# In-projection in two chunks of 1024 columns instead of four of 512

## The chip, the cores and the metric

The kernel runs on one core of a Trainium2 chip. TensorE multiplies matrices (PE in the profile; PEld is its loading of the stationary operand), VectorE (DVE), ScalarE (ACT) and GpSimd (POOL) do the elementwise work, and SyncE (SP) issues most transfers. The metric is the device time of one execution in microseconds; lower is better. Times are compared as medians of several runs, and one execution is profiled instruction by instruction.

## The reference

One encoder layer on 1024 tokens of width 1024, all in float32. Only its first step is changed here:

```python
hn = rms_norm(x, norm1_g)
proj = hn @ w_in                      # (1024, 1024) @ (1024, 2304): qA 512 | kA 128 | vA 128 | qB 512 | kB 512 | vB 512
qa, ka = rope(rms_norm(qa, gain)), rope(rms_norm(ka, gain))   # per head of 64
qb, kb = rms_norm(qb, gain), rms_norm(kb, gain)
```

After it come dense attention for group A (8 query heads on 2 key heads), a mixture of dilated window attentions for group B, an output projection with two RMSNorms, and a GEGLU MLP with a centred width-3 convolution. The row factor of the first RMSNorm isn't applied to x: the norms of q and k take it up in their epsilon, and v is scaled by it later. The column gain norm1_g is multiplied into the weights.

## The kernel before

**Precision.** Each float32 operand is split into a high part (ACT copies it into a rounded type) and a low part (DVE subtracts). A product is three matmuls: high x high, high x low, low x high. So each k-tile of 128 rows and each tile of 128 tokens costs three matmuls, with 128x128 of x as the stationary operand and the weights as the moving one.

**Strassen-Winograd products.** The kA and vA columns (256) are done first, in plain form, one tile of 128 tokens after the other (`kv_proj`, L287). The other four blocks of 512 columns are `CHUNKS`: kb, vb, qa, qb. In each chunk tokens, inner dimension and columns are halved, and seven products of halves with sums and differences of blocks (`prods`, L240) replace the eight block products. A product therefore has 512 tokens (4 tiles), 4 k-tiles and 256 columns: 4 x 4 x 3 = 48 matmuls of 256 moving columns; the four chunks have 28 products. The x side is prepared once (`x_sums`, L256, and `s_split`, which splits them), the weight side for each product (`w_prep`, L392: a difference of two blocks on DVE, a copy on ACT, a subtraction on DVE, 1024 columns each) into one of three buffers, two products ahead. Weights arrive in two transfers of 1 MB per chunk (`w_load`) and are scaled by norm1_g in place, on ACT, the first two pieces on GpSimd (`w_scale`, L381).

**Results.** A product fills 1024 columns of PSUM (two banks); there are three such groups (`in_group`, L412). `in_out` (L434) copies or adds it into the chunk's quadrants c11 to c22, with DVE or ACT on 1024 columns at a time and two of the first chunk's sums on GpSimd. When a quadrant is final, `done` (L471) yields its next steps: for kb a square, mean, root, norm and the store to a scratch in DRAM; for vb the scaling and the store; for qa a norm and the rotary turn (a table and eight small products on GpSimd, then two DVE operations); for qb the norm. The three last sums of the qb chunk and the later query norms are put into the attention's loop as `late` and `spread` steps (from L1283), tied to a place there by an operand.

**The mean square of x** is summed from eight row tiles of x loaded beside the transposed x (`n_load`, L263; `n_sq`, L266) through two buffers.

**Order.** The loop over m (L1194) writes the steps down in one order. A planner of the framework then orders each engine's queue from that order and from its own estimate of when operands are ready; each engine takes its queue strictly in turn. So an instruction whose operand comes later than planned holds up what is queued behind it on its engine. The attention's first groups follow directly: `a_main_bounded` (L721), scores, exponential on ACT, split, product with v. Its first group needs the rotated queries of tokens 0 to 511, heads 0 to 3, transposed on TensorE by the steps in `prep`.

The kernel holds a second form of the attention for data outside a bound, which isn't executed with these inputs.

Of the kernel before, what the change touches and what calls it, by code (L numbers as in the profile page):

```python
# [27 lines left out]
CHUNKS = (("kb", 1280), ("vb", 1792), ("qa", 0), ("qb", 768))  # L28
# [35 lines left out]
F_TMP = O_F  # L64
F_UA = O_F + 1024
F_WA = (O_F + 2048, O_F + 4096)
F_WC = O_F + 6144
F_XN = (O_F, O_F + 4096)
F_KVT = O_F + 5120
F_KSQ = O_F + 4096  # L70
# [66 lines left out]
def tile_encoder_layer(ctx, tc, x, xT, w_in, w_kv, gains, norm1_g, norm2_g, w_out, w_up, convs,  # L137
# [14 lines left out]
    def emit(bounded):  # L152
# [85 lines left out]

        chunks = [(at, kind) for kind, at in CHUNKS]
        prods = [(c, n) for c in range(4) for n in ((1, 5, 2, 7, 6, 3, 4) if c else (1, 2, 5, 7, 6, 3, 4))]  # L240
# [7 lines left out]

        def x_load_t(tt):
            dma(f(qab(tt), 1024), xT[:, tt, :])  # L250

        def x_prep(tt):
            for half in range(2):
                split(a_op(((1, 2), (3, 4))[tt // 4][half], tt % 4), f(qab(tt) + 512 * half, 512))

        def x_sums(tt):  # L256
            q0, q1 = qab(tt), qab(tt + 4)
            vec.tensor_tensor(f(q1 + 512, 512), f(q1, 512), f(q1 + 512, 512), op=OP.add)
            vec.tensor_tensor(f(q1, 512), f(q0, 512), f(q1, 512), op=OP.subtract)
            vec.tensor_tensor(f(q0, 512), f(q1 + 512, 512), f(q0, 512), op=OP.subtract)  # L260
            vec.tensor_tensor(f(q0 + 512, 512), f(q0 + 512, 512), f(q0, 512), op=OP.subtract)

        def n_load(tt):  # L263
            dma(f(F_XN[tt % 2], 1024), perm_rows(x, tt, D))

        def n_sq(tt):  # L266
            act(bank(4, 1024), f(F_XN[tt % 2], 1024), AF.Square, accum_out=f(SM_SS1 + tt, 1))
            if tt < 6:
                n_load(tt + 2)

        def s_split(n, t):
            raw = {5: qab(t + 4) + 512, 7: qab(t + 4), 6: qab(t), 3: qab(t) + 512}[n]
            split(a_op(n, t), f(raw, 512))


        def kv_load(half):
            dma(f(F_WC + 1024 * half, 1024), w_kv[half])

        def kv_split(k):
            o, raw, g = R_A[7] + 2048 * (k // 4) + 256 * (k % 4), f(F_WC + 256 * k, 256), f(SM_G1 + k, 1)  # L280
            act(r(o, 256), raw, AF.Copy, scale=g)
            vec.scalar_tensor_tensor(r(o + 1024, 256), raw, g, rf(o, 256), op0=OP.mult, op1=OP.subtract)

        def kv_bank(tt):
            return tt
# [16 lines left out]
        def kv_out(i):  # L302
            stg = F_KVT + 256 * (i % 3)
            act(f(stg, 256), bank(kv_bank(i), 256), AF.Copy)
            dma(kvscr[i], f(stg, 256))


        def k_fetch():
            dma(heads(f(F_TMP, 1024), 8), kvscr[:, :, 0:128].rearrange("t p c -> p t c"))

        def k_norm():
            k3, t = heads(f(F_TMP, 1024), 16), F_KSQ + 1024
            act(f(F_KSQ, 1024), f(F_TMP, 1024), AF.Square)
            vec.tensor_reduce(f(t, 16), heads(f(F_KSQ, 1024), 16), axis=AX.X, op=OP.add)
# [4 lines left out]
            vec.tensor_tensor(k3, k3, f(t, 16)[:, :, None].to_broadcast([128, 16, 64]), op=OP.mult)  # L319
            vec.tensor_tensor(k3, k3, fp(O_GA + 128, [0, 16], [1, 64]), op=OP.mult)  # L320

        def k_turn():
            for ax in range(2):
                for half in range(2):
                    gp.tensor_tensor(fp(F_KSQ + 32 * ax + 16 * half, [128, 8], [64, 2], [1, 16]),
                                     fp(F_TMP + 32 * ax + 16 * (1 - half), [128, 8], [64, 2], [1, 16]),
                                     fp(F_ROPE + 64 + 32 * ax + 16 * half, [128, 8], [0, 2], [1, 16]), op=OP.mult)

        def k_add():
            k4 = fp(F_TMP, [128, 8], [64, 2], [1, 64])  # L330
            vec.tensor_tensor(k4, k4, fp(F_ROPE, [128, 8], [0, 2], [1, 64]), op=OP.mult)
            vec.tensor_tensor(f(F_TMP, 1024), f(F_TMP, 1024), f(F_KSQ, 1024), op=OP.add)

        def k_split():
            src = fp(F_TMP, [64, 16], [1, 64])
            h, l = (64, 0) if bounded else (0, 64)
            act(rp(R_KNA + h, [128, 16], [1, 64]), src, AF.Copy)
            vec.tensor_tensor(rp(R_KNA + l, [128, 16], [1, 64]), src, rfp(R_KNA + h, [128, 16], [1, 64]), op=OP.subtract)
# [12 lines left out]

        def v_fetch():
            gp.memset(fp(F_VA + 64, [66, 16], [1, 2]), 1.0)
            for kv in range(2):
                dma(fp(F_VA + 66 * kv, [132, 8], [1, 64]),
                    kvscr[:, :, 128 + 64 * kv:192 + 64 * kv].rearrange("t p c -> p t c"))

        def v_scale():
# [3 lines left out]
            for t in range(8):  # L362
                v = fp(F_VA + 132 * t, [66, 2], [1, 64])
                act(v, v, AF.Copy, scale=f(SM_SS1 + t, 1))
            if bounded:
                act(r(R_VA, 1056), f(F_VA, 1056), AF.Copy)
                vec.tensor_tensor(r(R_VA + 1056, 1056), f(F_VA, 1056), rf(R_VA, 1056), op=OP.subtract)
# [7 lines left out]
        def w_buf(c, half):  # L375
            return F_WC if half else F_WA[c % 2]

        def w_load(c, half):
            dma(f(w_buf(c, half), 2048), w_in[c, half])

        def w_scale(c, half):  # L381
            for k in range(4):
                o, g = f(w_buf(c, half) + 512 * k, 512), f(SM_G1 + 4 * half + k, 1)
                if c or half or k > 1:
                    act(o, o, AF.Copy, scale=g)
                else:
                    gp.tensor_scalar(o, o, g, None, op0=OP.mult)

        def w_op(m):
            return R_WR + 2048 * (m % 3)  # L390

        def w_prep(m):  # L392
            if m >= len(prods):
                return
            c, n = prods[m]
            b11, b12, b21, b22 = [fp(w_buf(c, half) + 256 * u, [512, 4], [1, 256]) for half in range(2) for u in range(2)]
            eng = vec
            if n == 5:
                vec.tensor_tensor(b11, b12, b11, op=OP.subtract)
            elif n == 7:  # L400
                eng.tensor_tensor(b12, b22, b12, op=OP.subtract)
            elif n == 6:
                eng.tensor_tensor(b11, b22, b11, op=OP.subtract)
            elif n == 4:
                eng.tensor_tensor(b11, b21, b11, op=OP.subtract)
            src = {2: b21, 3: b22, 7: b12}.get(n, b11)
            o = w_op(m)
            h = rp(o, [256, 4], [1, 256])
            act(h, src, AF.Copy)
            vec.tensor_tensor(rp(o + 1024, [256, 4], [1, 256]), src, rfp(o, [256, 4], [1, 256]), op=OP.subtract)  # L410

        def in_group(m):  # L412
            c, n = prods[m]
            g = {1: 0, 2: 0, 3: 0, 5: 1, 6: 1, 7: 2, 4: 2}[n]
            return (0, 1024, 3072)[g if g == 2 else (g + c) % 2]

        def in_product(m, ts=range(4)):
            c, n = prods[m]
            w = w_op(m)
# [1519 lines left out]
```

## Time and profile before

| | |
|---|---|
| median of 3 runs | 1198.62 us (1197.52 to 1198.69) |
| profiled execution | 1198.82 us, span 1197.0 us |
| TensorE busy | 1178.0 us (98%) |
| DVE, ACT, POOL busy | 1009.3, 662.8, 338.9 us |
| in-projection on TensorE | k/v from 7.3 us; products from 22.1 to 198.7 us |
| in-projection products | 1344 matmuls of 256 columns |
| mean granted TensorE clock | 0.999 |

A row of a group reads: line, engine, operation, output <- input, shapes, count | busy us, mean ns of one | idle time of the engine before them and what ended it. Matmuls are pipelined and the printed durations of neighbours overlap. Rows of single instructions begin with start and duration in us.

### The profile page before, as it was taken

How to read it: one execution, taken by the hardware profiler on the slowest of the kernel's cores; microseconds unless marked ns; L12 is line 12 of the kernel's file. 1: busy time of each engine (PE TensorE's matmuls, PEld its weight loads, DVE VectorE, ACT ScalarE, POOL GpSimd, SP SyncE). 2: the span in 40 equal slices, each digit the busy share in tenths (PEclk: the TensorE clock that was granted, in tenths of full speed). 3: DMA queues.
4: the chain of work that ended last, by engine and by line, in shares of the span. 5: the costliest groups of instructions: out<-in, count | busy, mean ns of one | idle time of the engine just before them, and what ended most of it. 6: DMA issues, size and time to landing. Idle time of an engine off the chain costs nothing.

```text
span 1197.0 us, 17588 instructions
## 1 busy us (share of the span) xinstructions
PE 1178.0 (98%) x6548; PEld 999.8 (84%) x6548; DVE 1009.3 (84%) x1364; ACT 662.8 (55%) x964; POOL 338.9 (28%) x236
## 2 busy tenths in 40 slices
PE   7999999999999999999999999999999999999998
PEld 7999998666669998887788888888888888888886
DVE  6988587989988888657999999999999997966663
ACT  6866546889887778336544443434344363543331
POOL 1010122320024430011465555646556514000000
PEclk9999999999999999999999999999999999999999
DMA  8446301020015655322223232332323267967872
GB/s 322 135 136 152 96 1 42 6 54 18 9 36 123 148 117 176 124 71 97 73 86 106 97 114 88 108 111 103 121 79 113 93 215 270 357 206 243 297 232 77
DMA packets 118778, 151.20 MB, mean 126 GB/s; under 512 B 51360, under 2 KB 78752, under 8 KB 117664
## 3 DMA queue, kind: packets, MB, share of 16 engines
q1 hardware_dynamic: 116544, 144.27, 37.1%
q0 software_dynamic: 2144, 5.77, 2.2%
q8 instruction: 52, 0.85, 0.3%
q14 instruction: 38, 0.31, 0.1%
HBM read 111.47 MB, written 33.82 MB: 121 GB/s over the span
## 4 chain that ended last, share of the span: by engine, by line
PE 87%; DVE 3%; ACT 1%; POOL 1%; issue 1%; DMA 0%; ACTq 0%; POOLq 0%; DVEq 0%
PE ps L1575 11%; PE ps L1573 11%; PE ps L1574 11%; PE ps L735 6%; PE ps L1716 6%; PE ps L1715 6%; PE ps L1717 6%; PE ps L426 3%; PE ps L427 3%; PE ps L428 3%; PE ps L964 3%; PE ps L999 2%; PE ps L1106 2%; PE ps L1104 2%; PE ps L1105 2%; PE ps L751 2%
## 5 line engine op out<-in xcount | busy, mean ns | idle before, releaser
L1573 PE MATMUL ps<-bigr 128*128 128x512 f32 x616 | 239.8, 390 | 0.5 <-ACT bigr L1158 0.5
L1574 PE MATMUL ps<-bigr 128*128 128x512 f32 x616 | 239.6, 389 | 0.0
L1575 PE MATMUL ps<-bigr 128*128 128x512 f32 x616 | 239.6, 389 | 0.0
L1612 DVE SCALAR_TENSOR_TENSOR bigf<-bigf 128x768 f32<-128x768 f32 (+1 forms) x176 | 193.4, 1135 | 0.7
L1541 ACT ACTIVATE bigr<-bigf 128x512 fp32r<-128x512 f32 x154 | 91.7, 623 | 141.6 <-POOL bigf L1533 109.3
L1695 ACT ACTIVATE bigr<-bigf 128x1024 fp32r<-128x1024 f32 (+1 forms) x99 | 83.6, 867 | 115.7 <-PE ps L1717 66.7
L1573 PEld LDWEIGHTS ps<-bigr 128*128 128x128 f32 x616 | 115.6, 188 | 24.7 <-ACT bigr L1158 0.9
L1574 PEld LDWEIGHTS ps<-bigr 128*128 128x128 f32 x616 | 115.6, 188 | 24.1
L1575 PEld LDWEIGHTS ps<-bigr 128*128 128x128 f32 x616 | 115.6, 188 | 24.0
L427 PE MATMUL ps<-bigr 128*128 128x256 f32 x448 | 126.9, 283 | 1.4 <-DVE bigr L410 1.4
L426 PE MATMUL ps<-bigr 128*128 128x256 f32 x448 | 127.1, 284 | 0.1
L428 PE MATMUL ps<-bigr 128*128 128x256 f32 x448 | 126.8, 283 | 0.0
L1696 DVE TENSOR_TENSOR bigr<-bigf,bigr 128x1024 fp32r<-128x1024 f32 (+1 forms) x99 | 97.6, 1005 | 27.5 <-ACT bigr L1695 25.6
L1715 PE MATMUL ps<-bigr 128*128 128x512 f32 x308 | 119.8, 389 | 0.0
L1716 PE MATMUL ps<-bigr 128*128 128x512 f32 x308 | 119.8, 389 | 0.0
L1717 PE MATMUL ps<-bigr 128*128 128x512 f32 x308 | 119.8, 389 | 0.0
L1542 DVE TENSOR_TENSOR bigr<-bigf,bigr 128x512 fp32r<-128x512 f32 x112 | 106.1, 949 | 3.1 <-ACT bigr L1541 2.8
L735 PE MATMUL ps<-bigr 128*66 128x512 f32 x384 | 99.9, 394 | 0.0
L427 PEld LDWEIGHTS ps<-bigr 128*128 128x128 f32 x448 | 86.0, 192 | 1.6 <-DVE bigr L410 1.6
L426 PEld LDWEIGHTS ps<-bigr 128*128 128x128 f32 x448 | 86.0, 192 | 0.4 <-ACT bigf L441 0.4
L762 DVE TENSOR_TENSOR bigr<-bigf,bigr 128x1024 fp32r<-128x1024 f32 x64 | 80.8, 1269 | 6.4 <-ACT bigr L761 5.7
L428 PEld LDWEIGHTS ps<-bigr 128*128 128x128 f32 x448 | 86.0, 192 | 0.0
(218 smaller groups left out, 2450.5 us busy)
## 6 DMA issues: line engine op xcount, KB each, us to landing
bigf<-w_down SPq DMA_DIRECT2D x99, 256.0 KB, 4.2
bigf<-w_up SPq DMA_DIRECT2D x44, 512.0 KB, 3.5
bigf<-gscr SPq DMA_DIRECT2D x77, 256.0 KB, 4.2
gscr<-bigf SPq DMA_DIRECT2D x31, 512.0 KB, 2.6
bigf<-w_in SPq DMA_DIRECT2D x8, 1024.0 KB, 5.7
bigf<-x SPq DMA_DIRECT2D x16, 512.0 KB, 4.6
bigf<-xT SPq DMA_DIRECT2D x8, 512.0 KB, 7.6
bigf<-w_out SPq DMA_DIRECT2D x8, 512.0 KB, 3.6
```

Of the source, the lines that this page charges most:

```text
L426: mm(o, ah, wh, start=(k == 0 and t % 2 == 0 and n != 2), stop=False, skip_group_check=True)
L427: mm(o, ah, wl, start=False, stop=False, skip_group_check=True)
L428: mm(o, al, wh, start=False, stop=(k == 3), skip_group_check=True)
L735: mm(bank(ob)[0:66], r(w, 66), r(p + 512 * u, 512), start=(kt == 0 and i == 0), stop=(kt == 7 and i == 2))
L1542: low = lambda eng: eng.tensor_tensor(rp(o + 512, [128, 4], [1, 128]), src, rfp(o, [128, 4], [1, 128]), op=OP.subtract)
L1573: mm(bank(b), wh, th, start=(k == 0 and n in (1, 5, 6, 7)), stop=False, skip_group_check=True)
L1574: mm(bank(b), wh, tl, start=False, stop=False, skip_group_check=True)
L1575: mm(bank(b), wl, th, start=False, stop=(k == 3), skip_group_check=True)
L1612: vec.scalar_tensor_tensor(f(a + o, n), f(i + d, n), w_, f(a + o, n), op0=OP.mult, op1=OP.add)
L1715: mm(o, ah, r(d, 512), start=(q == 0 and n in (1, 5, 2)), stop=False, skip_group_check=True)
L1716: mm(o, ah, r(d + 1024, 512), start=False, stop=False, skip_group_check=True)
L1717: mm(o, al, r(d, 512), start=False, stop=(q == NQ - 1), skip_group_check=True)
```

## The change

There are two chunks of 1024 columns, (kb, vb) and (qa, qb), each with seven products of 512 tokens x 512 x 512 columns. A product is worked in four units, one per k-tile, each of 4 token tiles x 3 matmuls of 512 moving columns; a token tile has one PSUM bank, so a product fills half of PSUM (banks 0 to 3 or 4 to 7), and the products take the halves by turns. The weights of a unit (one k-tile, 512 columns high and 512 low) are one of six slots of a ring and are prepared four units ahead; scaling by norm1_g is folded into the split of products 1 and 2 and into the differences, and ACT scales only two of four blocks beforehand. Weight blocks have three places, and a block is loaded slice by slice where the one before it has been used. The products' order is 1, 5, 2, 3, 6, 7, 4 in the first chunk and 1, 5, 2, 6, 7, 4, 3 in the second, with another sequence of sums; all of these are on DVE and ACT, 512 columns at a time. The last product (qb only) runs token tile by token tile. The k/v tiles 4 to 7, formerly behind products 0 and 1, all stand behind the first product. The x tiles are stored with their halves exchanged for tokens 512 to 1023; row tiles of x come through a single buffer, in which the rotary table is loaded later. Steps for q, k and v are written down by unit number (`at(m, ...)`). In the attention the three leftover sums are gone, and the norm multiplication of the two query groups of tokens 512 to 1023 is there instead.

```diff
-CHUNKS = (("kb", 1280), ("vb", 1792), ("qa", 0), ("qb", 768))
+CHUNKS = ((("kb", 1280), ("vb", 1792)), (("qa", 0), ("qb", 768)))
...
-        prods = [(c, n) for c in range(4) for n in ((1, 5, 2, 7, 6, 3, 4) if c else (1, 2, 5, 7, 6, 3, 4))]
+        ORDER = ((1, 5, 2, 3, 6, 7, 4), (1, 5, 2, 6, 7, 4, 3))
+        prods = [(c, n) for c in range(2) for n in ORDER[c]]
...
         def n_load(tt):
-            dma(f(F_XN[tt % 2], 1024), perm_rows(x, tt, D))
+            dma(f(F_ROPE, 1024), perm_rows(x, tt, D))
 
         def n_sq(tt):
-            act(bank(4, 1024), f(F_XN[tt % 2], 1024), AF.Square, accum_out=f(SM_SS1 + tt, 1))
-            if tt < 6:
-                n_load(tt + 2)
+            act(f(F_ROPE, 1024), f(F_ROPE, 1024), AF.Square, accum_out=f(SM_SS1 + tt, 1))
...
         def w_op(m):
-            return R_WR + 2048 * (m % 3)
+            return R_WR + 1024 * (m % 6)
 
         def w_prep(m):
-            if m >= len(prods):
+            if m >= 4 * len(prods):
                 return
+            c, n = prods[m // 4]
+            k = m % 4
+            b11, b12, b21, b22, b4 = [f(w_at(c, b, k), 512) for b in ("11", "12", "21", "22", "21b")]
+            g0, g1 = f(SM_G1 + k, 1), f(SM_G1 + 4 + k, 1)
+            if n == 5:
+                act(b12, b12, AF.Copy, scale=g0)
+                vec.scalar_tensor_tensor(b11, b11, f(F_NG + k, 1), b12, op0=OP.mult, op1=OP.add)
+            if n == (6 if c else 3):
+                act(b22, b22, AF.Copy, scale=g1)
+            if n == 6:
+                vec.tensor_tensor(b11, b22, b11, op=OP.subtract)
+            if n == 7:
+                vec.tensor_tensor(b12, b22, b12, op=OP.subtract)
+            if n == 4:
+                vec.scalar_tensor_tensor(b11, b4, g1, b11, op0=OP.mult, op1=OP.subtract)
+            src, o = {1: b11, 2: b21, 3: b22, 7: b12}.get(n, b11), w_op(m)
+            if n in (1, 2):
+                act(r(o, 512), src, AF.Copy, scale=(g0, g1)[n - 1])
+                vec.scalar_tensor_tensor(r(o + 512, 512), src, (g0, g1)[n - 1], rf(o, 512), op0=OP.mult, op1=OP.subtract)
+            else:
+                act(r(o, 512), src, AF.Copy)
+                vec.tensor_tensor(r(o + 512, 512), src, rf(o, 512), op=OP.subtract)
+
+        def in_bank(c, n):
+            return 4 * ((ORDER[c].index(n) + c + 1) % 2)
+
+        def in_unit(m, ts=range(4)):
+            c, n = prods[m // 4]
+            k, w = m % 4, w_op(m)
+            for t in ts:
+                a = a_op(n, t) + 128 * k
+                o = bank(in_bank(c, n) + t)
+                mm(o, r(a, 128), r(w, 512), start=(k == 0 and n != 2 and (c == 1 or n != 3)), stop=False, skip_group_check=True)
+                mm(o, r(a, 128), r(w + 512, 512), start=False, stop=False, skip_group_check=True)
+                mm(o, r(a + 512, 128), r(w, 512), start=False, stop=(k == 3), skip_group_check=True)
...
+        at(11, mean_x)
+        at(18, dma, f(F_ROPE, 1024), rope)
...
+        for k in range(4):
+            for m, c, b in ((7, 0, "22"), (16, 0, "21b"), (17, 1, "11"), (22, 1, "12"), (24, 1, "21"), (32, 1, "22"), (40, 1, "21b")):
+                at(m + k, w_load, c, b, k, 1)
...
+        for i, s in enumerate(qa[0][0][4:]):
+            at(48 + i // 3, s)
+        for m in (51, 51, 52):
+            at(m, take, prep, 1)
...
+        for m in range(4 * len(prods)):
+            c, n = prods[m // 4]
+            if m < 52:
+                in_unit(m)
             else:
...
+                for k in range(4):
+                    in_unit(52 + k, [m - 52])
+                in_out(13, m - 52)
+            if m % 4 == 3 and m < 52:
+                for t in range(4):
+                    in_out(m // 4, t)
             if m == 3:
...
+                for i in range(4, 8):
+                    kv_tile(i)
+                    n_sq(i - 4)
+                    n_load(i - 3)
+            w_prep(m + 4)
+            for s in steps.pop(m, []):
+                s()
```

More of the change, by code (lines that the diff above doesn't have):

```diff
@@ L1 @@
+from collections import defaultdict
 from contextlib import ExitStack
@@ L256, in x_sums @@
[L256 to L261, printed above, removed]
+                split(a_op(((1, 2), (3, 4))[tt // 4][half], tt % 4), f(x_at(tt, half), 512))
@@ L372, in fill_k @@
                     bias=0.0 if bounded else -1.0)
[L375 to L387, printed above, removed]
+        place = ({"11": 0, "12": 2, "21": 1, "22": 1, "21b": 1}, {"11": 2, "12": 1, "21": 0, "22": 0, "21b": 1})
```

443 lines of the change are left out of this document (191 added, 252 removed).

## The prediction

> **What bounds the kernel now.** I read the page's first part, then TensorE's waits, then the busy time by stretches, then the groups of the in-projection, and last the single rows.
>
> ```profile
> span 1197.0 us, 17588 instructions
> PE 1178.0 (98%) x6548; PEld 999.8 (84%) x6548; DVE 1009.3 (84%) x1364; ACT 662.8 (55%) x964; POOL 338.9 (28%) x236
> ...
> PE ps L292 <- ACT bigr L281: 7.3, 1, 7.3
> PE ps L427 <- DVE bigr L410: 1.4, 1, 1.4
> PE ps L740 <- DVE bigf L745: 1.3, 1, 1.3
> ```
>
> TensorE works 98% of the span. Its waits add up to little: 7.3 us at the start for the first operands, one of 1.4 us inside the in-projection and one of 1.3 us in the attention. So a faster stage shows in the end only if TensorE itself needs less time for it.
>
> ```profile
> 100.00:120.00 20.00, 20.00 (x169) 20.00 (x169) 17.81 (x20) 11.71 (x21) 1.95 (x2) 1.00 0.54 139
> 120.00:140.00 20.00, 20.00 (x169) 20.00 (x168) 10.38 (x8) 10.34 (x12) 2.97 (x4) 1.00 0.23 68
> 160.00:180.00 20.00, 18.63 (x156) 18.42 (x156) 16.83 (x27) 13.46 (x20) 0.96 (x3) 1.00 0.00 1
> ...
> 560.00:1100.00 540.00, 537.78 (x2376) 444.70 (x2375) 500.67 (x596) 242.59 (x345) 237.00 (x134) 1.00 0.41 141
> ```
>
> Columns: stretch, its length, then busy time and count of PE, PEld, DVE, ACT, POOL, the granted clock, the DMA share and GB/s. In the in-projection (first three rows) TensorE is full although DVE is at 10.38 of 20 us in one of them: nothing feeds it too slowly, and the clock is 1.00. The fourth row is the MLP, whose matmuls are 512 wide: 540 us hold 2376 of them, 0.227 us each, and the weight loads (PEld) leave room there, while in the in-projection they fill the whole stretch.
>
> ```profile
> 22.13 0.28 PE L426 MATMUL ps<-bigr 128*128 128x256 f32 x1
> ...
> 99.94 0.28 PE L426 MATMUL ps<-bigr 128*128 128x256 f32 x1
> ...
> 101.86 0.28 PE L427 MATMUL ps<-bigr 128*128 128x256 f32 x1
> ...
> 198.73 0.40 PE L751 MATMUL ps<-bigr 128*128 128x512 f32 x1
> ...
> 699.78 0.39 PE L1574 MATMUL ps<-bigr 128*128 128x512 f32 x1
> ...
> 703.86 0.39 PE L1574 MATMUL ps<-bigr 128*128 128x512 f32 x1
> ...
> L426 PE MATMUL ps<-bigr 128*128 128x256 f32 x448 | 127.1, 284 | 0.1
> L427 PE MATMUL ps<-bigr 128*128 128x256 f32 x448 | 126.9, 283 | 1.4 <-DVE bigr L410 1.4
> L428 PE MATMUL ps<-bigr 128*128 128x256 f32 x448 | 126.8, 283 | 0.0
> ```
>
> The printed durations overlap; the pitch between starts is what counts. 256 wide: 16 steps in 1.92 us, 0.1200 us. 512 wide: 18 steps in 4.08 us, 0.2267 us. The difference, 0.1067 us for 256 more columns, leaves 0.0133 us per matmul that doesn't depend on its width. The first and the third row (L426, L751) are the stage's first product and the attention's first score.
>
> **The change part by part.** *Matmuls.* 3 x 448 = 1344 products 256 wide become 672 that are 512 wide, with the same operands in total (2 chunks x 7 products x 4 k-tiles x 4 row tiles x 3 terms). Before: 1344 x 0.1200 = 161.3 us. After: 672 x 0.2267 = 152.3 us. That is **-8.96 us** on the path that sets the end, since TensorE is full in this stage. I take the 512 row of the MLP because operand type, shape and memory are the same; from the other side, pitches that merely double would give 0. The Trainium skill, page "TensorE: Matmul & The Clock Gate", section "Back-to-back issue gap", gives a warm gap of N/2.4 ns plus about 2.5 ns; by it the estimate would be 672 x 2.5 ns = 1.7 us of gain instead. The trace speaks against it at both widths: 120.0 and 226.7 ns where it gives 109 and 216.
>
> *The wait of 1.4 us.* Its story:
>
> ```profile
> 156.58 4.39 POOL L298 TENSOR_TENSOR bigf<-bigf 128x128 f32<-128x128 f32 x6 [0.53 <-DVE bigf L438]
> 161.00 1.06 ACT L500 ACTIVATE bigf<-bigf 128x1024 f32<-128x1024 f32 x1 [6.82 <-POOL bigf L298]
> 161.96 1.04 ACT L409 ACTIVATE bigr<-bigf 128x1024 fp32r<-128x1024 f32 x1
> 166.92 1.22 DVE L410 TENSOR_TENSOR bigr<-bigf,bigr 128x1024 fp32r<-128x1024 f32 x1
> 168.19 0.38 PE L427 MATMUL ps<-bigr 128*128 128x256 f32 x1 [1.37 <-DVE bigr L410]
> ```
>
> A square of the query norm stood 6.82 us on ACT behind GpSimd's rotation, and the weight split queued after it came late. In the new order the first queries are rotated only in units 48 to 50 of 56 (a unit is one k-tile of one product, 12 matmuls, 2.72 us), so this place is empty: **-1.37 us** (0 if another such place opens).
>
> *Weight preparation.* Instead of 28 splits of 1024 columns two products ahead there are 56 of 512, four units ahead in a ring of six; scaling by the norm gain goes into the split or into the DVE operation of products 1, 2, 5 and 4. Lookahead is 4 x 2.72 = 10.9 us. Where nothing else is queued, DVE takes 0.65 us for 512 columns (20.7 / 32 below), so one unit costs 0.65 or, with a sum, 1.3 us of DVE against 2.72 us of TensorE.
>
> ```profile
> L410 DVE TENSOR_TENSOR bigr<-bigf,bigr 128x1024 fp32r<-128x1024 f32 x28 | 34.1, 1218 | 15.0 <-ACT bigr L409 15.0
> L247 DVE TENSOR_TENSOR bigr<-bigf,bigr 128x512 fp32r<-128x512 f32 x32 | 20.7, 688 | 7.5 <-ACT bigr L246 7.5
> L438 DVE TENSOR_TENSOR bigf<-ps,bigf 128x1024 f32<-128x1024 f32 x16 | 19.5, 1219 | 4.0 <-ACT bigf L449 2.1 <-PE ps L428 1.9
> L438 DVE TENSOR_TENSOR bigf<-bigf 128x1024 f32<-128x1024 f32 x9 | 13.9, 1585 | 2.1 <-POOL bigf L298 2.0
> L298 POOL TENSOR_TENSOR bigf<-bigf 128x128 f32<-128x128 f32 x16 | 10.7, 699 | 16.2 <-issue 12.8 <-DVE bigf L438 3.4
> L519 DVE TENSOR_TENSOR bigf<-bigf 128x1024 f32<-128x1024 f32 x8 | 9.8, 1222 | 0.1
> L504 DVE TENSOR_REDUCE bigf<-bigf 128x16 f32<-128x1024 f32 x8 | 9.7, 1210 | 3.2 <-ACT bigf L500 3.1
> ```
>
> *DVE by product.* The sums of products are 44 operations of 512 (28.6 us) instead of 25 of 1024 (33.4 us). The fullest product is the fourth of the second chunk (6, units 40 to 43): 8 operations of weight work and 8 of sums, 16 x 0.65 = 10.4 us, and two query norms of about 3.3 us each (a reduction 1.21, a multiplication 1.22, small ones), 17.0 us in 10.9 us of TensorE. DVE is then 6.1 us behind. The product before it needs 5.2 us, the two behind it some 10. A backlog of 6.1 us lies under the 10.9 us of lookahead, and the same 10.9 us stand between a product's sums and the next use of its PSUM half. So I cost the new grain and the halves by turns at **0**; without that cover it would be the 6.1 us.
>
> *x rows.* The mean square of x is taken from eight row tiles through one buffer instead of two: load, square, load.
>
> ```profile
> 30.00:40.00 10.00, 10.00 (x85) 10.00 (x85) 10.00 (x16) 8.54 (x18) 0.00 (x0) 1.00 0.27 85
> 40.00:80.00 40.00, 40.00 (x336) 40.00 (x335) 34.76 (x45) 32.19 (x50) 5.76 (x2) 1.00 0.45 154
> ...
> 41.15 1.03 ACT L267 ACTIVATE ps<-bigf 128x1024 f32<-128x1024 f32 x1 [0.61 <-DMA bigf<-x]
> ...
> bigf<-x SPq DMA_DIRECT2D x8, 512.0 KB, 4.5
> bigf<-xT SPq DMA_DIRECT2D x8, 512.0 KB, 7.6
> ```
>
> A turn is 4.5 + 1.03 us, say 5.7 with the read of the sum. The first square comes behind the first product and one k/v tile, near 22.1 + 10.9 + 24 x 0.12 = 36 us; seven turns later it is 76 us. The first norms need the result and are dealt to units 12 and 13; unit 12 ends at 22.1 + 13 x 2.72 + 96 x 0.12 = 69 us. They come some 7 us late, less than the lookahead, and the weight splits don't depend on them. Each load may hold ACT some 0.6 us, as it does now. On SP the next weight slices and the stores of k and v stand behind a waiting load of x; the tightest slices (block 22, asked for in units 7 to 10, split in 8 to 11, used in 12 to 15) still have five units from the issue to the use. **0**, from 0 to the slower case below.
>
> *Start.* The first product needs half as much weight (1 MB) before it begins, and GpSimd's scaling is gone, but now it starts with no wait behind the k/v matmuls, so there is nothing to win; x tiles arrive in two pieces per partition, which touches the 7.3 us. **0** (-0.3 to +1.0).
>
> *The end of the stage.* Rotation of the first query group writes where the last weights lay, so it begins after the split of unit 51, emitted behind unit 47.
>
> ```profile
> 235.22 2.47 POOL L522 TENSOR_TENSOR bigf<-bigf 128x512 f32<-128x512 f32 x1 [7.17 <-DVE bigf L1307]
> 237.76 4.71 POOL L298 TENSOR_TENSOR bigf<-bigf 128x128 f32<-128x128 f32 x8
> 242.51 1.22 DVE L529 TENSOR_TENSOR bigf<-bigf 128x1024 f32<-128x1024 f32 x1 [2.03 <-POOL bigf L298]
> ...
> 247.06 0.68 DVE L745 COPY bigf<-ps 66x512 f32<-66x512 f32 x1
> 247.79 0.46 PE L740 MATMUL ps<-bigf 66*128 66x66 f32 x4 [1.28 <-DVE bigf L745]
> ```
>
> Table and turns 7.2 us, two DVE operations 2.4 us, the split of the queries 0.8 us: 10.4 us. TensorE's transposes of that group stand after the first quarter of the last product, five units or 13.6 us later, and the attention queues behind them. With DVE 6.1 us behind the chain takes 16.5 us. So 0 to 2.9 us; **+1.0**, nearer the low end, since the backlog falls to about 5 us by then and part of it is other work.
>
> *Attention.* The three sums left over from the last chunk go away, and two of the late query groups bring their norm multiplication (1.22 us) with them. In the rows above GpSimd's rotation already kept DVE 2.03 us and that TensorE 1.28 us; a norm ahead of it makes it 1.2 us later. **+1.2** (-1.3 if the shift of everything empties the place, +2.4 if both groups pay).
>
> **Sum.** -8.96 - 1.37 + 1.0 + 1.2 = -8.1 us. The profiled execution took 1198.82 us (span 1197.0), 0.2 us above the median of 1198.62; 1198.82 - 8.1 = 1190.7, and by the median **1190.5 us**.
>
> **Rivals.** *Every handover is hidden:* no cost at the end of the stage, and the 1.3 us in the attention goes too. 1198.6 - 8.96 - 1.37 - 1.3 = 1187.0. For it: 3 us of DVE work fewer in the sums. Against: the attention's DVE is full whatever comes before.
>
> *DVE becomes the bound:* the two heavy places (products 3, 6 of the first chunk, 6 of the second) are paid each time, since in-order engines stand behind one another as in the 6.82 us above: 6.1 us plus about as much from the first chunk's k norms, less what a quiet product gives back, some 8 us. 1198.6 - 10.3 + 8 = 1196.3, from 1194 to 1199. For it: 84% DVE already; against: DVE was full from 30 to 40 us (row above) and TensorE had no wait there.
>
> *Slower:* the chain of x rows through one buffer. If a load takes not 4.5 but 8 us, as xT's 7.6 us shows is possible when queues are full, seven turns are 3.5 us longer each, 24.5 us. The norms wait on DVE in order, with the weight splits behind them; 10.9 us are covered, 13.6 us reach TensorE: 1198.6 - 10.3 + 13.6 + 1 = 1203. From a load of 7.5 us on (21.2 us late, 10.3 through) the gain is gone, from 7.9 us on it is slower by 2.4. Against: DMA is at 0.45 share from 40 to 80 us, and x loads already run there at 4.5 us.
>
> *Matmuls don't gain as said:* the 13.3 ns come from the in-projection's place, not its width, and only about 1.7 us is won (this is also what the page's gap would make of it). 1198.6 - 1.7 - 1.4 + 2.2 = 1197.7.
>
> **How the numbers follow.** Forecast 0.54, all hidden 0.14, DVE bound 0.14, slower 0.14, no gain per matmul 0.04. A measurement of this kernel tells about 0.2%, 2.4 us, from no change: faster is below 1196.2. The forecast, the first rival and half of the second are faster, 0.75; the other half and the last are the same, 0.11; the third is slower, 0.14. The likeliest case's own range is 1187.5 to 1194. The range to 8 in 10 takes in both rivals on its sides, 1186 to 1198.5.
>
> **What would show it.** After: 672 rows 128x512 in the in-projection, pitch 0.227 us, weight loads no longer full; the first score matmul (now 198.73 us) near 189.5. Wrong if the pitch is above 0.235; if TensorE waits for a weight split or a PSUM half (DVE bound) more than 3 us in total; if ACT or DVE stand over 3 us behind loads of x (slower case); if transposes wait for the query split over 3 us at the end of the stage. In the attention, the wait for L745's counterpart near 237 us shows the norm's cost.

## The result and the profile after

The changed kernel takes 1192.51 us (median of 5 runs, 1191.56 to 1193.01) against 1198.62 us for the one before (median of 5, 1197.52 to 1199.01). The ratio is 0.995 with a 95% interval of 0.9935 to 0.9964: faster, by 6.1 us. The forecast was 1190.5 us, so 2.0 us of the expected 8.1 us are missing. The profiled span fell by 6.2 us, from 1197.0 to 1190.8.

The first part of the page of the changed kernel, then TensorE's waits (us in total, times, longest):

```profile
span 1190.8 us, 16352 instructions
PE 1170.1 (98%) x5876; PEld 963.7 (81%) x5876; DVE 1010.8 (85%) x1430; ACT 661.2 (56%) x986; POOL 332.0 (28%) x236
...
PE ps L299 <- ACT bigr L288: 7.7, 1, 7.7
PE ps L299 <- ACT bigr L246: 2.8, 3, 1.7
...
PE ps L745 <- DVE bigf L750: 1.0, 1, 1.0
PE ps L756 <- DVE bigf L451: 0.8, 1, 0.8
...
PE ps L756 <- ACT bigr L670: 0.4, 1, 0.4
```

TensorE is busy 7.9 us less. The wait of 1.4 us in the in-projection is gone. New are three waits, 2.8 us together, for the split of x tiles (L246), and one of 0.8 us for a DVE sum (L451). The first score matmul starts at 192.31 us, 6.4 us earlier than before (198.73) but later than the forecast's 189.5.

The same kernel by stretches, with one of the three product groups and two of its single rows:

```profile
0.00:40.00 40.00, 29.04 (x166) 25.36 (x167) 25.62 (x56) 26.04 (x50) 0.20 (x4) 1.00 0.76 264
40.00:180.00 140.00, 140.00 (x665) 117.55 (x664) 119.99 (x211) 89.65 (x161) 14.13 (x22) 1.00 0.44 124
180.00:200.00 20.00, 18.74 (x88) 14.58 (x87) 16.19 (x33) 13.24 (x19) 5.83 (x9) 1.00 0.08 27
...
59.20 0.39 PE L437 MATMUL ps<-bigr 128*128 128x512 f32 x1
63.96 0.39 PE L437 MATMUL ps<-bigr 128*128 128x512 f32 x1
...
L437 PE MATMUL ps<-bigr 128*128 128x512 f32 x224 | 87.4, 390 | 0.0
```

From 40 to 180 us TensorE has no gap at all, and the weight loads take 117.55 of 140 us, no longer all of it. The two single rows lie 21 matmuls apart: 4.76 / 21 = 0.2267 us of pitch. So the middle of the stage went as planned; what is missing was lost before 40 us and after 180 us.

The rows behind the new wait at the start, in the timeline of the changed kernel: the transfers of x tiles 1 to 3 (one row) and 4 to 7 on SP's queue, splits on ACT, and TensorE's rows that wait for a split, with the first k/v matmul of tiles 4 to 7 as the last row (the bracket is the idle time and what ended it):

```profile
2.73 1.46 SPq L254 DMA_DIRECT2D bigf<-xT  x3
...
13.89 0.38 SPq L254 DMA_DIRECT2D bigf<-xT  x1
18.30 0.38 SPq L254 DMA_DIRECT2D bigf<-xT  x1
23.13 0.38 SPq L254 DMA_DIRECT2D bigf<-xT  x1
28.27 0.38 SPq L254 DMA_DIRECT2D bigf<-xT  x1
...
23.18 1.14 ACT L246 ACTIVATE bigr<-bigf 128x512 fp32r<-128x512 f32 x2
28.27 1.15 ACT L246 ACTIVATE bigr<-bigf 128x512 fp32r<-128x512 f32 x2 [1.25 <-DMA bigf<-xT]
33.39 1.68 ACT L246 ACTIVATE bigr<-bigf 128x512 fp32r<-128x512 f32 x3 [0.89 <-DMA bigf<-xT]
...
23.85 0.39 PE L299 MATMUL ps<-bigr 128*128 128x256 f32 x1 [1.66 <-ACT bigr L246]
28.95 0.39 PE L299 MATMUL ps<-bigr 128*128 128x256 f32 x1 [0.37 <-ACT bigr L246]
34.07 0.38 PE L299 MATMUL ps<-bigr 128*128 128x256 f32 x1 [0.80 <-ACT bigr L246]
...
37.46 0.28 PE L299 MATMUL ps<-bigr 128*128 128x256 f32 x1
```

The four transfers of tiles 4 to 7 are a chain: each is issued when the one before it lands, 4.4 to 5.1 us a link. The load issued at 18.30 us (tile 5) lands at 23.13, that of tile 6 at 28.27, and that of tile 7 by 33.39 us. At these three moments ACT begins a split that TensorE waits for.

The waiting matmuls are not those of tiles 4 to 7. TensorE does 48 k/v matmuls (tiles 0 and 1) from 7.66 us, 24 of the first product from 16.58 us, then from 23.85 to 37.23 us the other 48 k/v matmuls of tiles 0 to 3 mixed with the rest of the first product. The 96 of tiles 4 to 7 follow from 37.46 us without a wait. So tiles 2 and 3 wait, which stood ahead of the products in the kernel before as well. Their own loads were issued by 4.19 us, and the issue at 13.89 us waits for the landing of the last of them. In the program built from this kernel, the split of the first half of tile 2 waits for the load of tile 5, that of the first half of tile 3 for the load of tile 6, and that of the second half of tile 2 for the load of tile 7, though none of them reads what these loads bring. In the kernel before, where each tile is one contiguous piece, the loads of tiles 4 to 7 were issued in pairs at 10.84 and 15.09 us, and the k/v matmuls of tiles 0 to 3 ran on from the second one without a wait.

The end of the stage, DVE and TensorE in the timeline of the changed kernel:

```profile
192.32 1.21 DVE L517 TENSOR_TENSOR bigf<-bigf 128x1024 f32<-128x1024 f32 x1
193.46 1.27 DVE L451 TENSOR_TENSOR bigf<-ps,bigf 128x512 f32<-128x512 f32 x2
...
192.31 0.39 PE L756 MATMUL ps<-bigr 128*128 128x512 f32 x1
194.19 0.50 PE L756 MATMUL ps<-bigr 128*128 128x512 f32 x1 [0.82 <-DVE bigf L451]
```

A score matmul of the attention needs a PSUM bank that the last product still occupies. The sum that frees it (L451) stands on DVE behind a query norm (L517). That norm was written down for a later place in the attention; its operands were ready, and the planner drew it ahead.

### The profile page after: what moved, and what is told of

It is laid out like the page before. It is cut to its first block, busy times and chain, and to the rows that moved or that the text cites. A ratio compares the mean times of both kernels' runs of the same rounds, so it can differ in the third digit from the quotient of the medians.

```text
span 1190.8 us, 16352 instructions
## 1 busy us (share of the span) xinstructions
PE 1170.1 (98%) x5876; PEld 963.7 (81%) x5876; DVE 1010.8 (85%) x1430; ACT 661.2 (56%) x986; POOL 332.0 (28%) x236
## 4 chain that ended last, share of the span: by engine, by line
PE 88%; DVE 5%; DMA 2%; ACT 2%; POOL 1%; issue 1%; SPq 0%; ACTq 0%; DVEq 0%; POOLq 0%
PE ps L1562 12%; PE ps L1561 12%; PE ps L1560 12%; PE ps L740 6%; PE ps L1704 6%; PE ps L1702 6%; PE ps L1703 6%; PE ps L439 3%; PE ps L437 3%; PE ps L438 3%; PE ps L969 3%; PE ps L1004 2%; PE ps L1109 2%; PE ps L1111 2%; PE ps L1110 2%; PE ps L756 2%
## 5 line engine op out<-in xcount | busy, mean ns | idle before, releaser
L1560 PE MATMUL ps<-bigr 128*128 128x512 f32 x616 | 239.8, 390 | 0.5 <-ACT bigr L1163 0.5
L1561 PE MATMUL ps<-bigr 128*128 128x512 f32 x616 | 239.6, 389 | 0.0
L1562 PE MATMUL ps<-bigr 128*128 128x512 f32 x616 | 239.6, 389 | 0.0
L1560 PEld LDWEIGHTS ps<-bigr 128*128 128x128 f32 x616 | 115.7, 188 | 25.0 <-ACT bigr L1163 0.9
L1562 PEld LDWEIGHTS ps<-bigr 128*128 128x128 f32 x616 | 115.7, 188 | 24.0
L1561 PEld LDWEIGHTS ps<-bigr 128*128 128x128 f32 x616 | 115.7, 188 | 23.8
L1702 PE MATMUL ps<-bigr 128*128 128x512 f32 x308 | 119.8, 389 | 0.0
L1703 PE MATMUL ps<-bigr 128*128 128x512 f32 x308 | 119.8, 389 | 0.0
L1704 PE MATMUL ps<-bigr 128*128 128x512 f32 x308 | 119.8, 389 | 0.0
L437 PE MATMUL ps<-bigr 128*128 128x512 f32 x224 | 87.4, 390 | 0.0
L438 PE MATMUL ps<-bigr 128*128 128x512 f32 x224 | 87.2, 389 | 0.0
L439 PE MATMUL ps<-bigr 128*128 128x512 f32 x224 | 87.1, 389 | 0.0
L1565 DVE TENSOR_TENSOR bigf<-ps,bigf 128x512 f32<-128x512 f32 x110 | 75.1, 682 | 5.1 <-PE ps L1562 4.8
L1529 POOL TENSOR_TENSOR bigr<-bigf,bigr 128x512 fp32r<-128x512 f32 x42 | 67.0, 1594 | 32.9 <-ACT bigr L1528 31.9
L740 PEld LDWEIGHTS ps<-bigr 128*66 128x66 f32 x384 | 50.9, 136 | 29.8
```

The lines of the kernel that those rows point to most:

```text
L437: mm(o, r(a, 128), r(w, 512), start=(k == 0 and n != 2 and (c == 1 or n != 3)), stop=False, skip_group_check=True)
L438: mm(o, r(a, 128), r(w + 512, 512), start=False, stop=False, skip_group_check=True)
L439: mm(o, r(a + 512, 128), r(w, 512), start=False, stop=(k == 3), skip_group_check=True)
L740: mm(bank(ob)[0:66], r(w, 66), r(p + 512 * u, 512), start=(kt == 0 and i == 0), stop=(kt == 7 and i == 2))
L1529: low = lambda eng: eng.tensor_tensor(rp(o + 512, [128, 4], [1, 128]), src, rfp(o, [128, 4], [1, 128]), op=OP.subtract)
L1560: mm(bank(b), wh, th, start=(k == 0 and n in (1, 5, 6, 7)), stop=False, skip_group_check=True)
```

## The experiments

Each is the changed kernel with one edit, unless it says otherwise. Medians go with the ratio to the kernel before.

### Loads of x tiles 4 to 7 without the chain

```diff
-            dma(fp(a, [b - a, 2], [1, 512]), heads(xT[:, tt, :], 2))
+            if tt > 3:
+                dma(f(a, 512), xT[:, tt, 0:512])
+                dma(f(b, 512), xT[:, tt, 512:1024])
+            else:
+                dma(fp(a, [b - a, 2], [1, 512]), heads(xT[:, tt, :], 2))
```

> The changed kernel, but each x tile of tokens 512 to 1023 comes in two transfers of 512 columns (one per half), so that no load of x has to wait for the one before it to land. Theory (the four loads of one strided transfer each stand in a chain, about 4.9 us a link, and TensorE's 3.1 us of waits between 20 and 36 us come from the last links): these waits go, span 1190.8 - 2.8 = 1188.0 us, time about 1189.7. Rival (the transfers fill the DMA engines there, share 0.92 to 0.96, so the tiles can't come sooner): span 1190.8 within 0.5, x tile 7 still lands near 33 us.

Measured: 1189.42 us (1187.81 to 1191.23), ratio 0.992 (0.9906 to 0.9933), span 1186.4. The first and the last of its eight transfers for tiles 4 to 7, and its waits of 0.4 us and more within the first 200 us:

```profile
12.57 0.33 SPq L255 DMA_DIRECT2D bigf<-xT  x1
...
17.51 0.43 SPq L256 DMA_DIRECT2D bigf<-xT  x1
...
PE ps L303 <- ACT bigr L292: 7.3, 1, 7.3
...
PE ps L760 <- DVE bigf L455: 0.8, 1, 0.8
...
PE ps L760 <- ACT bigr L674: 0.4, 1, 0.4
PE ps L441 <- ACT bigf L315: 0.4, 1, 0.4
```

All eight are issued within 5 us, and TensorE no longer waits for the split of x. A small wait for a k/v copy (L441 behind ACT's L315) is there instead, 0.4 us here and 0.8 us in the second run below. The k/v matmuls of tiles 0 to 3 now run from 8.14 to 20.86 us without a gap, ahead of the first product. So the waits come from the form of these four transfers (two separated pieces of 512 per partition in one instruction, with pieces of other tiles between them), not from the queue or the bandwidth. In the program the edit takes away both the chain and the waits of the splits of tiles 2 and 3 for later loads; the run doesn't tell their shares apart. Why the framework sees these transfers as overlapping stays open: tiles 0 to 3 come in two pieces too, and were issued within 2.9 us without waiting for one another.

Two runs on one chip, to rule out that the gain came from elsewhere:

> The changed kernel as it is, on one chip with the next kernel, so that the two can be compared there. Both theories of the start say 1192.5 us, with TensorE's waits for the split of x tiles 4 to 7 (line 299 behind ACT's line 246) at 2.8 to 3.4 us.

> x tiles 4 to 7 again as two contiguous transfers each, beside the changed kernel on the same chip. Theory (the chained loads cost TensorE some 3.1 us): 1189.4 us, 3.1 below the run beside it. Rival (most of the 3.1 us between the first two measurements was the varying slow phase of TensorE at the beginning, worth up to 1.1 us, and another chip): 1191 us or more, less than 2 below the run beside it.

Measured: 1192.96 us (1192.34 to 1193.59) for the changed kernel, with waits of 3.2 us behind L246; 1188.85 us (1188.17 to 1190.21) with the free loads, without such a wait. The difference is 4.1 us, spans 1191.1 and 1186.9. The rival falls. The theory's 3.1 us is lower than the measured 4.1 us: besides the waits, the first matmul started 0.4 us earlier (7.30 against 7.70 us), and the slow phase of TensorE described below was shorter. Both vary from run to run, so only the wait, about 3 us, is put down to the form of the loads. This version beats both kernels; against the one before it is 0.9918 (0.9904 to 0.9931).

### Products of 256 columns again

```diff
+                for u in range(2):
+                    o = bank(in_bank(c, n) + t, 256, 256 * u)
-                mm(o, r(a, 128), r(w, 512), ...)
+                    mm(o, r(a, 128), r(w + 256 * u, 256), ...)
...
```

> The changed kernel, but every matmul of the products is done as two of 256 columns (1344 instead of 672, all else the same). Theory (13.3 ns per matmul whatever its width): 672 x 13.3 ns = 8.96 us more, span 1199.7 us, pitch 0.120 us. Rival (only some 2.5 ns a matmul): 1.7 us more, 1192.5. Second rival (the gain of the change came from its new order, not from the width): within 1 us of 1190.8.

Measured: 1200.59 us, ratio 1.0009 (0.9999 to 1.0018), span 1199.2, 8.4 us above the changed kernel. The medians differ by 8.1 us, and by 7.6 us when each is set against the kernel before on its own chip. The pitch is 0.120 us again. The width alone is worth the whole gain and a little more. The rival of 1.7 us falls, and so does the rival of the new order. With the first falls, as a measure for this stream, the formula of the Trainium skill's page "TensorE: Matmul & The Clock Gate", section "Back-to-back issue gap", which would give those 1.7 us; the page itself calls it the gap of an isolated matmul, which the prediction didn't say. Two things blur the 8.4: the wait for L451 (0.8 us) isn't there, and in this execution a wait of 2.53 us that ended at 24.34 us brought the clock down for a while (see the last section).

### No chain of x rows

```diff
-            act(f(F_ROPE, 1024), f(F_ROPE, 1024), AF.Square, accum_out=f(SM_SS1 + tt, 1))
+            act(f(F_ROPE, 1024), f(F_ROPE, 1024), AF.Square, scale=0.2 if tt else 1.0, accum_out=f(SM_SS1 + tt, 1))
...
-            if i < 7:
-                at(2 * i - 3, n_load, i + 1)
...
-                    n_load(i - 3)
```

Seven of the eight loads of x rows are left out (each later square reads what the one before it left in the buffer, times 0.2), so the row factor's value is another.

> The changed kernel with only the first of the eight loads of x rows; the mean square is taken eight times from that tile (so its value is wrong), and no square waits for a transfer. Theory (the chain through one buffer lies under the lookahead): the in-projection after 40 us is as long as before, span 1190.8 less at most 0.5, plus what the 3.5 MB less of transfers free at the start (at most the 3.1 us of waits for x tiles, if these are short of bandwidth rather than in a chain). Rival (the chain reaches TensorE): waits for weight splits or PSUM vanish and the span falls by 2 us or more after 40 us.

Measured: 1192.28 us (four runs, 1190.37 to 1193.93), ratio 0.9941 (0.9926 to 0.9956), span 1192.0. TensorE still waits 3.4 us for the split of x tiles, once for 2.62 us, after which the granted clock is 0.60 from 24 to 28 us. By estimate that is 0.4 x 4 = 1.6 us and covers the 1.2 us by which the span of this execution, the slowest of the four, is longer. So the x rows cost nothing that shows beside this spread, and the waits for x tiles stay without them. The "slower" rival had its mechanism in the wrong chain: there is one that delays TensorE, but it is that of the loads of the transposed x at the start.

### More work on DVE

```diff
-                vec.tensor_tensor(r(o + 512, 512), src, rf(o, 512), op=OP.subtract)
+                for _ in range(3 if n == 7 else 1):
+                    vec.tensor_tensor(r(o + 512, 512), src, rf(o, 512), op=OP.subtract)
```

> The changed kernel, but the low part of the weights of product 7 is computed three times instead of once in both chunks: 8 more subtractions of 512 columns on DVE (4.8 us) in each of the two fullest stretches. Theory (a backlog of DVE lies under the four units of lookahead, 10.9 us): no more than 0.5 us longer, span 1190.8 to 1191.3. Rival (DVE bounds these stretches): each extra microsecond reaches TensorE, 5 to 10 us longer, 1196 to 1200.

Measured: 1195.36 us, ratio 0.9967 (0.9955 to 0.9979), span 1193.6, 2.8 us above the changed kernel: more than the theory's 0.5 and less than the rival's 5, so both miss. The groups of DVE's low splits, before (the changed kernel, L426) and with the edit (L427), then stretches and new waits of the edited one:

```profile
L426 DVE TENSOR_TENSOR bigr<-bigf,bigr 128x512 fp32r<-128x512 f32 x40 | 26.9, 688 | 8.7 <-ACT bigr L425 8.6
```

```profile
L427 DVE TENSOR_TENSOR bigr<-bigf,bigr 128x512 fp32r<-128x512 f32 x56 | 38.1, 704 | 4.1 <-ACT bigr L425 3.9
...
60.00:160.00 100.00, 100.00 (x443) 82.84 (x442) 90.44 (x168) 62.27 (x105) 6.06 (x8) 1.00 0.43 120
...
180.00:190.00 10.00, 8.24 (x39) 6.52 (x38) 8.54 (x15) 4.37 (x7) 1.43 (x4) 1.00 0.12 45
...
PE ps L192 <- DVE bigr L650: 1.8, 1, 1.8
...
PE ps L439 <- DVE bigr L427: 0.7, 1, 0.7
```

Sixteen more operations are 11.2 us of DVE. Those of the first chunk vanish (TensorE full from 60 to 160 us with DVE at 90.44 of 100). Those of the second come out as 0.7 us for a weight split and 1.8 us for the query split (L192 behind L650). The second is what the prediction feared for the end of the stage: the transposes of the first query group wait for DVE's backlog. It showed with some 5.6 us more of it than the changed kernel has; less was not tried. The waits for x tiles, which the edit doesn't touch, are 0.9 us longer in this execution (3.7 against 2.8), so DVE's share of the 2.8 us is put at the 2.5 us of the two new waits.

### What the wait at the end of the stage hangs on

First, the table loads. ACT switches its function table three times between 187.59 and 190.73 us, and the last sums share the queue with them. The edit makes the early exponential read a result of the roots, so that it comes after them:

```diff
-        at(54, act, f(SM_T + 96, 1), rf(R_Q2A, 1), AF.Exp, 0.0, 0.0)
+        at(54, act, f(SM_T + 96, 1), f(SM_T + 80, 1), AF.Exp, 0.0, 0.0)
```

> The changed kernel, but the one-element exponential that loads ACT's table ahead of the attention reads the last query root, so that it comes behind the roots: one table load instead of three at the end of the in-projection. Theory (the last product leaves PSUM late because DVE waits for roots that stand behind table loads of 1.28 us each): TensorE's wait of 0.8 us for that sum goes, and part of the 0.4 us behind it; span 1189.6 to 1190.1. Rival (DVE is behind by its own work): span 1190.8 within 0.3, the wait stays at 0.8.

Measured: 1192.81 us, ratio 0.9948 (0.9935 to 0.9962). One table load is left at this place, and the wait behind L451 is 1.2 us, not shorter. The theory falls. The norm (L517) stands ahead of the last two sums here too, from 190.76 us.

Then the norm drawn ahead, left out (the queries of tokens 512 to 1023 in group A stay without it):

```diff
+                if kind == "qa" and t0:
+                    return
```

> The changed kernel without the norm multiplication of the two query groups of tokens 512 to 1023 (two DVE operations of 1.22 us left out, so those queries are not normed). Theory (the planner draws the first of them, whose operands are ready, ahead to 192.3 us, in front of the sums that free the last product's PSUM, and TensorE waits 0.8 us there): that wait goes, span 1189.6 to 1190.2; the attention is as it was. Rival (it costs in the attention, where it was written down, as predicted 1.2 us): TensorE's waits after 240 us get shorter by about 1 us. Second rival (it costs nothing): 1190.8 within 0.3, the wait of 0.8 us stays.

Measured: 1191.63 us (four runs, 1191.35 to 1192.52), ratio 0.994 (0.9925 to 0.9955), span 1190.7. The wait behind L451 is gone and TensorE is busy 19.56 us of 180 to 200 instead of 18.74. So the norm was its cause. The median is 0.9 us lower than the changed kernel's, and the profiled execution is the slowest of the four (the others' spans are 1189.5 to 1190.1), so its span doesn't show the 0.8 us. Its lines:

```profile
23.63 0.39 PE L299 MATMUL ps<-bigr 128*128 128x256 f32 x1 [2.60 <-ACT bigr L246]
...
24.00:28.00 4.00, 4.00 (x18) 3.30 (x17) 2.86 (x5) 2.79 (x6) 0.00 (x0) 0.64 0.93 259
180.00:200.00 20.00, 19.56 (x93) 15.29 (x92) 16.19 (x33) 14.30 (x19) 4.77 (x9) 1.00 0.09 27
...
PE ps L747 <- DVE bigf L752: 1.3, 1, 1.3
PE ps L971 <- DMA bigr<-bigr: 0.8, 2, 0.5
```

After a wait of 2.60 us the granted clock is 0.64 from 24 to 28 us, by estimate 0.36 x 4 = 1.4 us. Up to the first score that has been made up (192.00 against 192.31 us), since there is one wait for x tiles instead of three and the slow phase at the start was shorter. Behind the first score two waits in the attention, 0.3 and 0.8 us longer, take the 0.8 us back.

Last, with the free loads as well, the norm kept but tied to its place in the attention:

```diff
-            for ts, at in zip(roped, (...)):
-                spread[at[0]] = tick + run(ts[:-2])
+            for j, (ts, at) in enumerate(zip(roped, (...))):
+                spread[at[0]] = tick + run(ts[:-2], SM_T + 48 * (j - 1) if j else None)
```

> The kernel with free x loads (span 1186.4 us), and the late norm multiplications tied to their place in the attention by an operand, so that they can't be drawn ahead of the last sums. Theory (the norm drawn ahead is what the last sum waits for): TensorE's wait of 0.8 us for that sum goes, span 1185.6, if the attention doesn't give it back (up to 1.2 us by its own wait near 240 us). Rival (DVE is behind by its other work): 1186.4 within 0.3. The start varies by about 0.5 us between executions.

Measured: 1190.57 us (1190.14 to 1191.07), ratio 0.9931 (0.9918 to 0.9945), no better than the free loads alone. The wait behind the last sum is gone, and the attention has these:

```profile
PE ps L760 <- ACT bigr L674: 1.9, 2, 1.5
PE ps L749 <- DVE bigf L754: 1.6, 1, 1.6
...
PE ps L973 <- DMA bigr<-bigr: 0.7, 1, 0.7
```

Without the tie these places are 0.4, 0.9 and at most 0.2 us. With the tie the 0.8 us are moved, not won: the planner's early place is the cheaper one. The run before, without the norm's work, has the lower median; it isn't a gain open to the kernel.

### Narrower still: 128 columns

Four products of 128 columns in place of one of 512, in both chunks:

```diff
+                for u in range(4):
+                    o = bank(in_bank(c, n) + t, 128, 128 * u)
-                mm(o, r(a, 128), r(w, 512), ...)
+                    mm(o, r(a, 128), r(w + 128 * u, 128), ...)
...
```

> The changed kernel with every matmul of the products done as four of 128 columns (2688 instead of 672). Theory (streaming at 2.4 columns per ns and 13.3 ns per matmul at every width): pitch 66.7 ns, 672 x 40 ns = 26.9 us more, span 1217.7. Rival (a weight load has its own floor, near the 80 ns at which the 128-column transposes follow one another): pitch 80 ns, 62.7 us more, 1253.5. Second rival (the 120 ns of 256 columns are a floor of the weight load): pitch 120 ns, 170 us more, 1361.

Measured (one run): 1606.31 us, span 1604.5. All three expectations miss, since TensorE ran at half its clock from about 66 to 607 us, after a wait of 6.3 us. To tell the pitch from the clock, the same in the first chunk only:

```diff
+                q = 128 if c == 0 else 512
+                for u in range(512 // q):
+                    o = bank(in_bank(c, n) + t, q, q * u)
...
```

> Four products of 128 columns in place of one of 512, in the first chunk only (1344 matmuls instead of 336); the second chunk stays at 512. At full clock the pitch of 0.111 us seen before the clock fell would give 1344 x 0.111 - 336 x 0.2267 = 73 us more. Theory (the clock is lowered while the weight loads follow one another without a gap, and comes back soon after): most of the 1344 at 0.213 us, 286 - 76 = 210 us more, 1400 us, and a granted clock of 1.00 within some tens of us of the second chunk. Rival (once lowered, the clock stays at half for some 500 us): the second chunk's 336 at 0.427 us are 67 us longer too, 1470 us or more.

Measured (one run): 1395.51 us, span 1393.7, 202.9 us above the changed kernel, near the theory's 210. What the clock did is read below. At full clock the pitch of 128 columns is 0.112 us (10 steps in 1.12 us, first fence of the last section), not the 0.067 us that 13.3 ns beside the columns would give: below 256 columns something else sets the pace; what, is open. The weight loads are as full as TensorE there.

## Why the prediction was right or wrong

- **Matmuls, -8.96 us: right.** 672 matmuls at 0.2267 us, as the MLP's row said; the undone width costs 8.4 us of span, 7.6 to 8.1 by the medians. The 13.3 ns per matmul hold between 256 and 512 columns and fail at 128.
- **The wait of 1.4 us: right.** No such place opened between 40 and 180 us.
- **Weight preparation and DVE by product, 0: right.** DVE is 85% busy and nothing waits for it in the middle. The added work shows that the first chunk could carry 5.6 us more, and the second hardly any. Even with 11.2 us more on DVE the cost is at most 2.8 us, so the rival of a bound DVE, with its 8 us, is far.
- **x rows, 0: right.** Without the loads the median is the same within 0.3 us, in a spread of 3.6 us.
- **"Start. 0 (-0.3 to +1.0)": wrong, and the main cause of the 2 us.** The sentence that went wrong is "there is nothing to win; x tiles arrive in two pieces per partition, which touches the 7.3 us". I priced the two pieces at the first tiles alone, where they touch the 7.3 us, and didn't ask what else waits for these loads. The loads of tiles 4 to 7 came one after another, every 4.4 to 5.1 us, and splits of tiles 2 and 3, whose data had landed, stood behind those of tiles 5 to 7. So TensorE waited inside the k/v work that the change didn't move. The k/v tiles 4 to 7, which it did move, run without a wait. Cost: 2.8 us of waits behind ACT, 0.25 us behind DVE, and 0.34 us by a later first matmul (7.66 against 7.32), which varies between 7.16 and 7.70 in executions of kernels with the same start. The term was +3.4 instead of 0, and some 3.1 of it go with the form of the loads.
- **End of the stage, +1.0: right in size by luck, wrong in mechanism.** 0.82 + 0.44 us of waits against 0.3 before, but the transposes of the first queries didn't wait. A score matmul waited for a PSUM bank behind a norm drawn ahead. The feared mechanism exists: 5.6 us more DVE work in the second chunk brings it out.
- **Attention, +1.2: wrong in sign.** The wait is 1.0 us instead of 1.3, so -0.3. The norm that I put there was begun at 192.32 us, ahead of the last sums. I had taken the place in the program's text for the place in the queue.

The sum with the measured terms: -8.96 - 1.37 + 3.4 + 1.0 - 0.3 = -6.2 us, the difference of the spans. It fits better than it should: -8.96 is count times pitch, and a wait of 0.8 us in the kernel before (TensorE behind GpSimd's L644, at 343.75 us) is gone in the changed one without being in the sum. Of the rivals, "every handover is hidden" fails at the start and at the end of the stage; the slower rival named a chain of loads, but another one, and not this cost.

## What to carry to other kernels

When a change reshapes a load, write down when it is issued, when it lands and everything that waits for it, not only its own readers: a load in two separated pieces can be ordered behind its neighbours, and work on other tiles behind it. A term of "0, hidden" is worth no more than the name and the time of the work that hides it: where I had named both, it held. Work that is tied to nothing may be drawn ahead by the planner into the last gap before a handover, and here tying it back only moved the wait.

## What the runs showed of the hardware

After some waits TensorE's granted clock fell to half, and this changes what a wait costs. Stretches of the kernel with 128 columns in the first chunk (granted clock third from the right), and its single rows:

```profile
37.69 0.28 PE L441 MATMUL ps<-bigr 128*128 128x128 f32 x1
38.81 0.27 PE L442 MATMUL ps<-bigr 128*128 128x128 f32 x1
...
23.05 0.58 PE L299 MATMUL ps<-bigr 128*128 128x256 f32 x1 [2.72 <-ACT bigr L246]
66.89 0.47 PE L440 MATMUL ps<-bigr 128*128 128x128 f32 x1 [4.54 <-ACT bigf L311]
...
249.70 0.41 PE L441 MATMUL ps<-bigr 128*128 128x128 f32 x1
251.83 0.41 PE L442 MATMUL ps<-bigr 128*128 128x128 f32 x1
...
24.00:28.00 4.00, 4.00 (x20) 4.00 (x20) 2.27 (x4) 2.77 (x7) 0.00 (x0) 0.50 0.84 279
36.00:40.00 4.00, 4.00 (x38) 4.00 (x37) 3.87 (x8) 4.00 (x9) 0.00 (x0) 1.00 0.15 43
100.00:300.00 200.00, 200.00 (x939) 200.00 (x939) 38.94 (x61) 32.86 (x52) 0.00 (x0) 0.50 0.16 43
312.00:318.00 6.00, 6.00 (x20) 5.20 (x21) 3.24 (x5) 1.69 (x2) 0.00 (x0) 0.50 0.00 0
320.00:340.00 20.00, 20.00 (x90) 16.57 (x89) 19.25 (x37) 11.05 (x21) 6.07 (x8) 1.00 0.39 95
```

After the wait of 2.72 us the clock is 0.50; it is 1.00 again by 36 us, with narrow products running at full pitch. So narrow products with full weight loads didn't lower it there, which is where the theory of that run was wrong. After the wait of 4.54 us it stays at 0.50 for 250 us, while TensorE has no gap: 10 steps of 128 columns in 2.13 us. It rises between 318 and 320 us, some 5 us after the 512-wide products begin at 314.12 us. In the kernel with 128 columns in both chunks it rose some 2 us after the last narrow product (605.93 us). So behind this second wait the clock didn't come back during the narrow products, and came back when wide ones ran. Why the first drop ended and the second didn't isn't settled; wider k/v products ran among the narrow ones only at the first.

Over the executions, the longest wait for x tiles and the clock behind it: 1.66 us (changed kernel), 1.60, 1.45 and 2.47 us left the clock at 1.00; 2.53, 2.60, 2.62, 2.72 and 4.54 us brought it to 0.50 to 0.77 from 24 to 28 us. The waits for x tiles therefore stand just below a second cost, by estimate 1.4 us in the stretch quoted for the kernel without the late norm, part of which takes the place of later waits. The Trainium skill, page "TensorE: Matmul & The Clock Gate", part 1, tells of a gate that halves the clock after an idle window of about 3.4 us, and counts the window from no fixed point. The halving agrees; waits shorter than that, 2.53 to 2.72 us, sufficed here.

At the start of each kernel the k/v products run at a pitch of 0.213 us instead of 0.12, though the clock's row shows 1.00. The phase ended at 13.95 us in the changed kernel, at 13.84 before and between 10.9 and 14.0 in the other executions, 3.6 to 6.5 us after the first matmul. Its length makes up to 1.3 us of difference between two executions ((6.5 - 3.6) x (1 - 0.12 / 0.213)), as far as no wait behind it takes it up, so a difference of 1 us between two profiles of this kernel is not yet a finding.
